# A transformer step with three sequence mixers: both softmax maps of the differential attention side by side, two sets of query and key tiles, projections and recurrence products in another order

## Chip, cores and metric

One core of one Trainium2 chip runs the whole program. The metric is the device time of one execution in microseconds (us). "Row halves" are partitions 0 to 63 and 64 to 127 of TensorE's array: a matmul that contracts over 64 rows needs one of them only.

## What is computed

1024 positions, width 1024, fp32. Block 1 projects the modulated, normalised input `h` onto 6688 columns. They feed three mixers, whose outputs are projected, gated and added; an output projection and a dense MLP follow. Block 2 (softmax attention and a mixture of experts) isn't touched.

```python
# mixer A: 4 heads, each with two maps of 64 dimensions; v has 128 columns
scores = einsum('bhiqd,bhikd->bhiqk', q, k) * 64**-0.5      # i = 0, 1: the two maps
scores = scores - slopes * abs(t - s)
p = softmax(scores, axis=-1)
o = (p[:, :, 0] - lam * p[:, :, 1]) @ v                      # then an RMS norm

# mixers B (4 heads of 64) and C (4 heads of 32 for keys, 64 for values), in both directions
S_t = diag(a_t) S_{t-1} + k_t v_t^T ;  o_t = S_t^T q_t

# merge: a gate for each branch, 3 * 1024 of the projected columns
m = sigmoid(gA) * (oA @ WA) + sigmoid(gB) * (oB @ WB) + sigmoid(gC) * (oC @ WC)
```

## The kernel before, in words

Every product of projections and scores is made in three passes: an operand is split into a rounded fp32r part (`hi`, ScalarE) and its remainder (`lo`, VectorE), and hi·hi, hi·lo and lo·hi are added up in PSUM (`mm3`, L91 to L93). Weights arrive by DMA (`wraw`) and are split (`whi` L98, `wlo` L99). PSUM has eight banks: `mm` is two buffers of two banks (tiles named `ps`, `pA`, `mm`), `mb` takes one half of an `mm` buffer, `tp` has two single banks, **`po` and `pj` one bank each, with a single buffer**: their tiles are handed out in the order in which the code asks for them, and each waits until the one before it has been read.

The code is written as a program of tiles; a scheduler orders each engine's instructions by priorities, from dependencies and modelled costs. What is written inside `low_priority()` fills the gaps that the rest leaves on an engine, as far as its buffers allow.

Block 1 up to the output projection, in the order of the code:

- **Branch A** (`branch_a` L405, `diff_head` L453). For each pair of heads the values are projected (`proj_N2`, tiles `dv`), for each head 128 query and 128 key columns (`proj_T2`, two halves of 512 positions, an `mm` buffer). `q_stack` (L361, L362) writes query hi and lo one above the other on the 128 partitions (`daq`, one tile for each map), `k_stack` (L369 to L373) key hi and lo, with the copies that stacking wants done by 16 DMAs from SBUF to SBUF (L371, L373, `dak`). A map's scores are then hi·hi + lo·hi in one matmul over K=128 (L379) and hi·lo in a second (L381), for each half of 512 keys: four matmuls for each map and each of the eight blocks of 128 queries, t. Then, on VectorE, the distance penalty with a running maximum (L466), ScalarE's exponential (L469), VectorE's combination of the two maps (L476), TensorE's transposes (L396), their split (L98, L99), the product with the values into `po`, a norm (ones matmul L490 into `po`), and a store (L493).
- **Branch B** (`branch_b`): values by `proj_V`, then two groups of two heads. A group projects its query, gate and two forget columns (`proj_T2`, four `mm` buffers), makes log decays and their running sums (L538, L540), and calls `scan_group` (L545): decayed products of queries and keys on TensorE (`products`, L555), once for the whole and at seven levels of chunk lengths 64 to 1, each over the group's heads one after the other; the levels' operands are made on VectorE (L571 to L582), ScalarE (L575, L576) and GpSimd (L577), and each product is merged into a tile `A` per head by a predicated copy on VectorE (L584). States (L612, L616), outputs (L631, L635) and a norm (`head_norm_gate`, L647 into `po`) follow.
- **Branch C** (`branch_c`): the same with four heads of 32 in one group; its rank-16 gate is `plr`, `pz` (L729).
- **Gates and merge** (`mid()`, called in `branch_c`, but in `low_priority`): `gate_cols` projects the 24 blocks of 128 gate columns through `pj`, copies them to `gst` (L791) and stores them in DRAM. `merge_ab` projects the outputs of A and B (`pj<-oT`), with VectorE multiplying by the gate (L818) straight from `pj`. `merge_c` (`mm<-oC`) and the output projection (`mb<-whi,mT`) follow.

Of the kernel before, what the change touches and what calls it, by code (L numbers as in the profile page):

```python
# [26 lines left out]
class Kern:  # L27
# [379 lines left out]
    def branch_a(self, hT, oa, first):  # L407
        nc, tc, a = self.nc, self.tc, self.a
        W = a["w_in"]
        with ExitStack() as ctx:  # L410
# [24 lines left out]
            for hp in range(2):  # L435
                vt = [sp.tile([128, NT, 256], FR, name="dv%d" % i, tag="dv%d" % i) for i in range(2)]
                self.proj_N2(self.w256(W, 1024 + hp * 256) if hp else first, hT, lambda t2, p: self.split_into(
                    p, *[x[:, 2 * t2:2 * t2 + 2, :] for x in vt]), self.mb)
                for h in (2 * hp, 2 * hp + 1):
                    Q = [sp.tile([128, 1024], FR, name="daq%d" % i, tag="daq%d" % i) for i in range(2)]  # L440
                    KK = [[sp.tile([128, 1024], FR, name="dak%d%d" % (i, j), tag="dak%d%d" % (i, j))
                           for j in range(2)] for i in range(2)]
                    p = self.proj_T2(self.w128(W, h * 128), hT)
                    for i in range(2):
                        self.q_stack(p[64 * i:64 * i + 64], 64 * i, Q[i], -0.125)
                    p = self.proj_T2(self.w128(W, 512 + h * 128), hT)
                    for i in range(2):
                        self.k_stack(p[64 * i:64 * i + 64], 64 * i, *KK[i])
                    nc.vector.tensor_scalar(tab, tab, 0.25, None, op0=ALU.mult)
                    self.diff_head(sp, Q, KK, [x[:, :, (h % 2) * 128:(h % 2) * 128 + 128] for x in vt],  # L450
                                   tab, nlam, ones, gcol, oa, h)

    def diff_head(self, sp, Q, KK, V, tab, nlam, ones, gcol, oa, h):  # L453
        nc = self.nc
        for qr in range(4):
            pt = self.pt_tiles(sp, 2)
            rc = sp.tile([128, 2], F32, name="drc", tag="drc", bufs=2)
            for qi in range(2):
# [3 lines left out]
                for i in range(2):  # L462
                    p = self.mm("ps")
                    self.scores(p, Q[i], KK[i][0], KK[i][1], t)
# [77 lines left out]
    def scan_group(self, sp, q, kf, kb, cf, cb, V, nh, escale, out):  # L542
# [6 lines left out]
        A = [sp.tile([128, 8, 128], F32, name="A%d" % h, tag="A%d" % h) for h in range(nh)]  # L549
# [11 lines left out]
        products(xk, q, lambda h, p: nc.scalar.activation(A[h], p, AF.Copy))  # L561
# [1589 lines left out]
```

## Time and profile before

| | us |
|---|---|
| three runs | 4387.36, 4399.77, 4403.98 (median 4399.77) |
| the profiled execution | 4400.4 |
| its span | 4398.6 |
| TensorE busy | 3972.5 (90%) |
| VectorE / ScalarE / GpSimd busy | 2367.1 / 1837.5 / 1149.5 |
| from the first head's projections to the end of `mm<-oC` | 93 to 1281 |

Matmuls overlap in TensorE's pipeline, so a row's duration is longer than the distance to the next start; a row in the timeline with x8 is a run of eight. What a matmul costs is the distance between starts: 0.234 us for 512 columns of fp32r at the full clock. An fp32 product of 128 columns has two records. The granted clock (PEclk) is a share of full speed.

### The profile page before, as it was taken

How to read it: one execution, taken by the hardware profiler on the slowest of the kernel's cores; microseconds unless marked ns; L12 is line 12 of the kernel's file. 1: busy time of each engine (PE TensorE's matmuls, PEld its weight loads, DVE VectorE, ACT ScalarE, POOL GpSimd, SP SyncE). 2: the span in 40 equal slices, each digit the busy share in tenths (PEclk: the TensorE clock that was granted, in tenths of full speed). 3: DMA queues.
4: the chain of work that ended last, by engine and by line, in shares of the span. 5: the costliest groups of instructions: out<-in, count | busy, mean ns of one | idle time of the engine just before them, and what ended most of it. 6: DMA issues, size and time to landing. Idle time of an engine off the chain costs nothing. (4 is left out here: it accounts for less than half of the span.)

```text
span 4398.6 us, 56718 instructions
## 1 busy us (share of the span) xinstructions
PE 3972.5 (90%) x21637; PEld 3280.9 (75%) x21637; DVE 2367.1 (54%) x3984; ACT 1837.5 (42%) x3064; POOL 1149.5 (26%) x878
## 2 busy tenths in 40 slices
PE   6999989989989999999899988699795988996997
PEld 5788867768768888887799987566594877884664
DVE  6545575544544233334536674666438567746665
ACT  3444432523233212121436662255423667842554
POOL 2000021322153212123522221011124646730111
PEclk8999989877799999999899998799996999997998
DMA  4222251102152211112233323699610001036996
GB/s 165 60 61 66 80 181 39 54 20 95 60 200 82 63 44 53 44 53 68 76 99 80 94 85 105 256 369 360 194 42 15 19 8 57 20 100 254 370 362 226
DMA packets 314163, 514.32 MB, mean 117 GB/s; under 512 B 39318, under 2 KB 212769, under 8 KB 313892
## 3 DMA queue, kind: packets, MB, share of 16 engines
q1 hardware_dynamic: 304244, 475.58, 32.0%
q0 software_dynamic: 9648, 35.13, 3.2%
q8 instruction: 170, 2.79, 0.3%
q14 instruction: 101, 0.83, 0.1%
HBM read 418.87 MB, written 83.36 MB: 114 GB/s over the span
## 5 line engine op out<-in xcount | busy, mean ns | idle before, releaser
L98 ACT ACTIVATE whi<-wraw 128x1024 fp32r<-128x1024 f32 (+3 forms) x451 | 465.3, 1035 | 929.2 <-PE mm L92 258.7
L99 DVE TENSOR_TENSOR wlo<-wraw,whi 128x1024 fp32r<-128x1024 f32 (+1 forms) x354 | 450.9, 1277 | 635.6 <-ACT whi L98 607.8
L99 POOL TENSOR_TENSOR wlo<-wraw,whi 128x1024 fp32r<-128x1024 f32 (+3 forms) x97 | 227.8, 2349 | 1227.8 <-ACT whi L98 1157.4
L91 PE MATMUL mm<-h,whi 128*128 128x512 f32 x832 | 331.5, 400 | 8.0 <-DVE xq L649 4.2
L92 PE MATMUL mm<-h,whi 128*128 128x512 f32 x832 | 331.6, 399 | 2.9 <-POOL h L99 1.8
L93 PE MATMUL mm<-h,wlo 128*128 128x512 f32 x832 | 331.4, 399 | 1.1 <-POOL wlo L99 1.1
L1619 PE MATMUL pd<-wraw,se 128*128 128x512 f32 x512 | 237.3, 598 | 1.9 <-ACT se L1611 1.9
L91 PE MATMUL pgu<-whi,xe 128*128 128x512 f32 x512 | 216.4, 423 | 5.3 <-ACT xe L98 5.3
L92 PE MATMUL pgu<-wlo,xe 128*128 128x512 f32 x512 | 216.4, 423 | 0.0
L91 PE MATMUL py<-whi,mr 128*128 128x512 f32 x512 | 201.6, 394 | 9.2 <-DVE mr L921 8.1
L912 DVE TENSOR_TENSOR Y<-py,Y 128x1024 f32<-128x1024 f32 x112 | 137.0, 1224 | 133.4 <-PE py L93 133.4
L93 PE MATMUL pgu<-whi,xe 128*128 128x512 f32 x512 | 204.3, 399 | 0.0
L93 PE MATMUL py<-whi,mr 128*128 128x512 f32 x512 | 203.1, 397 | 0.0
L92 PE MATMUL py<-wlo,mr 128*128 128x512 f32 x512 | 202.4, 395 | 0.0
L396 PE MATMUL ptp<-ident,e 128*128 128x128 f32 x1280 | 181.9, 277 | 11.8 <-ACT pf L400 5.1
L91 PEld LDWEIGHTS mm<-h,whi 128*128 128x128 f32 x832 | 156.9, 189 | 47.7 <-issue 5.3
L1023 DVE TENSOR_REDUCE ast<-ps 128x1 f32<-128x1024 f32 x128 | 156.4, 1222 | 66.4 <-PE ps L93 47.1
L92 PEld LDWEIGHTS mm<-h,whi 128*128 128x128 f32 x832 | 157.2, 189 | 41.6 <-POOL h L99 2.3
L93 PEld LDWEIGHTS mm<-h,wlo 128*128 128x128 f32 x832 | 157.4, 189 | 40.2 <-POOL wlo L99 2.0
L91 PE MATMUL pj<-h,whi 128*128 128x512 f32 x384 | 160.0, 417 | 17.6 <-ACT gst L791 17.5
L396 PEld LDWEIGHTS ptp<-ident,e 128*128 128x128 f32 x1280 | 148.9, 142 | 27.0 <-ACT pf L400 11.6
L1619 PEld LDWEIGHTS pd<-wraw,se 128*128 128x128 f32 x512 | 97.6, 191 | 95.2 <-issue 84.3
(625 smaller groups left out, 11111.4 us busy)
## 6 DMA issues: line engine op xcount, KB each, us to landing
wraw<-in_moe_w_gate_dram SPq DMA_DIRECT2D x128, 512.0 KB
wraw<-in_moe_w_up_dram SPq DMA_DIRECT2D x128, 512.0 KB
wraw<-in_moe_w_down_dram SPq DMA_DIRECT2D x128, 512.0 KB
wraw<-in_mlp_w_dram SPq DMA_DIRECT2D x64, 512.0 KB
wraw<-in_w_in_dram SPq DMA_DIRECT2D x52, 512.0 KB
wad<-in_ada_w_dram SPq DMA_DIRECT2D x48, 512.0 KB
gD<-gst SPq DMA_DIRECT2D x24, 512.0 KB
wraw<-x SPq DMA_DIRECT2D x20, 512.0 KB
```

Source lines behind the costliest of these rows:

```text
L91: t.matmul(out, l[0], r[0], start=start, stop=False)
L92: t.matmul(out, l[0], r[1], start=False, stop=False)
L93: return t.matmul(out, l[1], r[0], start=False, stop=stop)
L98: nc.scalar.activation(hi, src, AF.Copy)
L99: (nc.gpsimd if leng == "pool" else nc.vector).tensor_tensor(lo, src, hi.bitcast(F32), op=ALU.subtract)
L396: nc.tensor.transpose(p[:, k, :], e[:, (4 * kg + k) * 128:(4 * kg + k + 1) * 128], self.ident)
L912: nc.vector.tensor_tensor(y, pv, y, op=ALU.add)
L1023: nc.vector.tensor_reduce(out=st[:, 0:1], in_=pv, axis=AX.X, op=ALU.min)
L1619: nc.tensor.matmul(p[:, h, :], sT[:, k, :], w[:, h * 512:(h + 1) * 512], start=k == 0, stop=k == 3)
```

## The change

1. Branch A: queries and keys of a head lie as they come out of the projection, map 0 on partitions 0 to 63 and map 1 on 64 to 127, as one hi and one lo tile each, two sets in rotation. `q_stack`, `k_stack` and their 16 DMAs go. The scores become three matmuls over K=64 for each half of 512 keys, written alternately for the two maps. Projections of heads 1 to 3 and of the second pair's values go through `pj` instead of `mm`.
2. `early()`, in low priority and ahead of branch A in the code: all projections of B and C (2080 columns) go through `pj` and `gst` to DRAM, and the branches load them by DMA.
3. `products`: heads in pairs, alternating, four chunks at a time; the four or two tiles `A` become one.
4. `merge_ab`: the first of two halves in `po`, the second in `pj`.

```diff
 # branch_a
-                    p, *[x[:, 2 * t2:2 * t2 + 2, :] for x in vt]), self.mb)
+                    p, *[x[:, 2 * t2:2 * t2 + 2, :] for x in vt]), self.pj if hp else self.mb)
                 for h in (2 * hp, 2 * hp + 1):
-                    Q = [sp.tile([128, 1024], FR, name="daq%d" % i, tag="daq%d" % i) for i in range(2)]
-                    KK = [[sp.tile([128, 1024], FR, name="dak%d%d" % (i, j), tag="dak%d%d" % (i, j))
-                           for j in range(2)] for i in range(2)]
-                    p = self.proj_T2(self.w128(W, h * 128), hT)
-                    for i in range(2):
-                        self.q_stack(p[64 * i:64 * i + 64], 64 * i, Q[i], -0.125)
...
+                    Q, K = [[sp.tile([128, 1024], FR, name="da%s%d" % (n, i), tag="da%s%d" % (n, i), bufs=2)
+                             for i in range(2)] for n in "qk"]
+                    for c0, T, s in ((0, Q, -0.125), (512, K, 1.0)):
+                        w = self.w128(W, c0 + h * 128)
+                        for g in range(2):
+                            p = self.pj() if h else self.mb()
+                            self.proj_T(w, hT, p, g)
+                            hi, lo = [x[:, g * 512:(g + 1) * 512] for x in T]
+                            nc.scalar.activation(hi, p, AF.Copy, scale=s)
+                            nc.vector.scalar_tensor_tensor(lo, p, s, hi.bitcast(F32), op0=ALU.mult, op1=ALU.subtract)
 # diff_head
-                for i in range(2):
-                    p = self.mm("ps")
-                    self.scores(p, Q[i], KK[i][0], KK[i][1], t)
+                ps = [self.mm("ps") for _ in range(2)]
+                for kh in range(2):
+                    for n, (x, y) in enumerate(((0, 0), (0, 1), (1, 0))):
+                        for i in range(2):
+                            hs = slice(64 * i, 64 * i + 64)
+                            nc.tensor.matmul(ps[i][:, kh, :], Q[x][hs, t * 128:(t + 1) * 128],
+                                             K[y][hs, kh * 512:(kh + 1) * 512], start=n == 0, stop=n == 2)
+                for i, p in enumerate(ps):
 # scan_group
-            for h in range(nh):
-                p = self.mm("pA").rearrange("p a (c j) -> p (a c) j", j=128)
-                for c in range(8):
-                    nc.tensor.matmul(p[:, c, :], xk[h * dk:(h + 1) * dk, c * 128:(c + 1) * 128],
-                                     xq[h * dk:(h + 1) * dk, c * 128:(c + 1) * 128], start=True, stop=True)
-                done(h, p)
+            for h in range(0, nh, 2):
+                for g in range(0, 8, 4):
+                    p = self.mm("pA").rearrange("p a (c j) -> p a c j", j=128)
+                    for c in range(4):
+                        for i in range(2):
+                            hs, cs = slice((h + i) * dk, (h + i + 1) * dk), slice((g + c) * 128, (g + c + 1) * 128)
+                            nc.tensor.matmul(p[:, i, c, :], xk[hs, cs], xq[hs, cs], start=True, stop=True)
+                    done(A[:, h:h + 2, g:g + 4, :], p)
 # branch_b (branch_c in the same way)
-            self.proj_V(self.w256(W, 2304), hT, V)
+            self.load_V(vD, V)
...
-                p = self.proj_T2(self.w128(W, 1536 + 128 * i), hT)
-                nc.scalar.activation(q, p, AF.Silu)
+                nc.scalar.activation(q, load(q, 0, i), AF.Silu)
 # merge_ab
-                    p = self.pj()
+                    p = self.pj() if h else self.po()
 # program; store_rows and store_cols project through pj, copy to gst on ScalarE, and store
+        def early():
+            self.store_rows(h, vB, 2304, sf, W)
+            for i in range(2):
+                for k, c in enumerate((1536, 1792, 2048, 2560)):
+                    self.store_cols(h, pB[256 * k + 128 * i:256 * k + 128 * i + 128, :], c + 128 * i, sf, W)
+            self.store_cols(h, pC[512:544, :], 3584, sf, W, 32)
+            for k, c in enumerate((2816, 2944, 3328, 3456)):
+                self.store_cols(h, pC[128 * k:128 * k + 128, :], c, sf, W)
+            self.store_rows(h, vC, 3072, sf, W)
+        with self.low_priority():
+            early()
         self.branch_a(h, oD, first)
```

**The scores on TensorE.** Before, in head 0 (`ps` the scores, `dak` and `daq` keys and queries, `pj` low-priority projections); four matmuls for one map, one block of queries:

```order
L93 MATMUL pj_5525<-h10_97,wlo_5495 128x512
L379 MATMUL ps_919<-dak00_639,daq0_637 128x512
L381 MATMUL ps_919<-dak01_640,daq0_637 128x512
L379 MATMUL ps_919<-dak00_639,daq0_637 128x512
L381 MATMUL ps_919<-dak01_640,daq0_637 128x512
L91 MATMUL pj_5525<-h10_97,whi_5494 128x512
```

Now, at the same place; `ps_2027` is map 0 on the lower row half, `ps_2028` map 1 on the upper:

```order
L93 MATMUL pj_480<-whi_424,h11_98 128x256
L470 MATMUL ps_2027<-dak0_1859,daq0_1857 128x512
L470 MATMUL ps_2027<-dak1_1860,daq0_1857 128x512
L470 MATMUL ps_2027<-dak0_1859,daq1_1858 128x512
L470 MATMUL ps_2027<-dak0_1859,daq0_1857 128x512
L470 MATMUL ps_2027<-dak1_1860,daq0_1857 128x512
L470 MATMUL ps_2027<-dak0_1859,daq1_1858 128x512
L470 MATMUL ps_2028<-dak0_1859,daq0_1857 128x512
L470 MATMUL ps_2028<-dak1_1860,daq0_1857 128x512
L470 MATMUL ps_2028<-dak0_1859,daq1_1858 128x512
L470 MATMUL ps_2028<-dak0_1859,daq0_1857 128x512
L470 MATMUL ps_2028<-dak1_1860,daq0_1857 128x512
```

The matmuls that the code writes alternately stand as six of one map and then six of the other. So it is in most blocks of queries; in others the two maps' runs are parted by low-priority work, and in a few they alternate. In the whole order the 384 score matmuls lie in 52 unbroken runs, with 94 changes from one half to the other inside them.

**The end of head 0 on TensorE.** Before, the projections of head 1 (`mm_1285`) stand around the last norm of head 0 (L490):

```order
L92 MATMUL mm_1285<-h11_98,whi_1281 128x512
L93 MATMUL mm_1285<-h10_97,wlo_1282 128x512
L490 MATMUL po_1177<-dsq_1205,ones_426 128x256
L91 MATMUL mm_1285<-h10_97,whi_1281 128x512
L92 MATMUL mm_1285<-h11_98,whi_1281 128x512
```

Now tiles of `early()`, `pj_727` and then `pj_761` to `pj_1581`, stand between head 0 and head 1 (its last norm is L498); the rows are head 0's last product with the values and what follows it:

```order
L93 MATMUL po_2425<-pt0_2344,dv1_1652 128x256
L491 MATMUL po_2425<-ident_74,drc_2346 128x128 x2
L91 MATMUL pj_727<-h10_97,whi_696 128x512
L92 MATMUL pj_727<-h11_98,whi_696 128x512
L93 MATMUL pj_727<-h10_97,wlo_697 128x512
```

From head 0's last norm on, 528 matmuls of 512 columns and 192 of 256 columns (the second V of `early()`), all into `pj`, stand there before the first projection of head 1, with nothing between them; 72 more of 512 columns, head 1's own projections, precede its first score.

**The end of branch C on TensorE.** Before, the norms (L647) stand among the merge's `pj<-oT`, as soon as their outputs are there:

```order
L91 MATMUL pj_7221<-oT0_6876,whi_7200 128x512
L92 MATMUL pj_7221<-oT1_6880,whi_7200 128x512
L647 MATMUL po_7932<-xq_7925,bones_4885 128x512
L93 MATMUL pj_7221<-oT0_6876,wlo_7201 128x512
L91 MATMUL pj_7221<-oT0_6876,whi_7200 128x512
```

Now all four of them (L658) stand behind the merge's last product, right ahead of `mm<-oC`:

```order
L93 MATMUL pj_7572<-oT0_7084,wlo_7527 128x512
L658 MATMUL po_8133<-xq_8130,bones_5576 128x512
L658 MATMUL po_8137<-xq_8130,bones_5576 128x512
L658 MATMUL po_8180<-xq_8177,bones_5576 128x512
L658 MATMUL po_8184<-xq_8177,bones_5576 128x512
L91 MATMUL mm_8220<-oC0_8201,whi_8211 128x512
```

`merge_ab` is asked for before the recurrence of C in the code, and now holds turns of `po`: the norms come after all of them. From the output projection on, both orders are the same but for a few swaps of neighbours.

## Rows read from the trace of the kernel before

**Rows 1.** Busy time of each engine by stage (start:end in us, length; then busy us and instructions of PE, PEld, DVE, ACT, POOL; PEclk, DMA share, GB/s): head 0's projections, branch A, then for B's first and second group: setup, levels, states and outputs; the same for C; the merge; `mm<-oC`.

```profile
93.00:123.00 30.00, 27.97 (x121) 22.18 (x120) 6.12 (x5) 6.63 (x8) 2.36 (x1) 1.00 0.28 76
123.00:533.00 410.00, 403.37 (x2202) 343.24 (x2201) 222.77 (x381) 184.42 (x320) 27.51 (x11) 1.00 0.21 60
533.00:645.00 112.00, 99.26 (x466) 80.83 (x464) 79.33 (x95) 34.20 (x39) 30.60 (x14) 0.92 0.65 203
645.00:714.00 69.00, 60.51 (x367) 52.47 (x367) 55.76 (x56) 20.37 (x22) 21.54 (x9) 0.87 0.13 39
714.00:759.00 45.00, 43.49 (x218) 33.76 (x218) 13.15 (x33) 7.29 (x11) 2.73 (x2) 0.93 0.16 48
759.00:832.00 73.00, 67.46 (x279) 52.38 (x279) 22.49 (x36) 38.49 (x42) 26.28 (x11) 0.98 0.19 60
832.00:887.00 55.00, 49.18 (x284) 45.64 (x283) 47.73 (x52) 23.25 (x23) 15.64 (x7) 0.66 0.09 29
887.00:918.00 31.00, 26.57 (x104) 18.73 (x102) 11.24 (x31) 3.44 (x5) 0.00 (x0) 0.50 0.00 1
918.00:1020.00 102.00, 92.60 (x451) 71.25 (x448) 34.75 (x54) 28.98 (x31) 32.17 (x15) 0.92 0.13 38
1020.00:1152.00 132.00, 127.23 (x615) 109.53 (x613) 79.75 (x74) 44.27 (x44) 26.41 (x11) 0.62 0.23 81
1152.00:1207.00 55.00, 51.08 (x258) 36.33 (x258) 25.95 (x69) 13.84 (x15) 10.74 (x5) 0.96 0.25 84
1207.00:1249.00 42.00, 33.62 (x127) 23.34 (x128) 14.45 (x16) 22.40 (x25) 16.68 (x8) 0.96 0.55 207
1249.00:1281.00 32.00, 23.50 (x83) 17.56 (x82) 20.01 (x17) 14.88 (x18) 21.34 (x11) 0.84 0.73 251
```

**Rows 2.** TensorE's groups between 50 and 1300 us, shapes apart (line, engine, operation, out<-in, rows x columns of the array, xcount | busy us, mean ns | idle before, releaser).

```profile
L91 PE MATMUL mm<-h,whi 128*128 128x512 f32 x320 | 129.3, 404 | 6.7 <-DVE xq L649 4.2 <-ACT hq L675 1.8 <-ACT whi L98 0.7
L379 PE MATMUL ps<-dak,daq 128*128 128x512 f32 x128 | 52.9, 414 | 5.6 <-DMA dak<-dak 5.2 <-DVE dst L466 0.4
L381 PE MATMUL ps<-dak,daq 128*128 128x512 f32 x128 | 50.5, 397 | 0.8 <-DMA dak<-dak 0.7
L396 PE MATMUL ptp<-ident,e 128*128 128x128 f32 x256 | 34.8, 272 | 0.0
L555 PE MATMUL pA<-xq,xk 64*128 64x128 f32 x448 | 69.0, 345 | 7.7 <-DVE xk L582 5.8 <-DVE A L584 1.8
L555 PE MATMUL pA<-xq,xk 32*128 32x128 f32 x448 | 77.1, 369 | 4.5 <-DVE A L584 4.5
```

**Rows 3.** TensorE's timeline (start us, length us, engine, line, operation, run; idle before and releaser in brackets) at four places: scores and transposes; low-priority projections with a `pj` tile's end and the next one's start in between, twice; and the start of B's products.

```profile
141.31 0.39 PE L379 MATMUL ps<-dak,daq 128*128 128x512 f32 x1
141.53 0.39 PE L381 MATMUL ps<-dak,daq 128*128 128x512 f32 x1
141.76 0.39 PE L379 MATMUL ps<-dak,daq 128*128 128x512 f32 x1
...
142.91 1.04 PE L396 MATMUL ptp<-ident,e 128*128 128x128 f32 x8
143.71 0.48 PE L379 MATMUL ps<-dak,daq 128*128 128x512 f32 x1
...
623.20 0.40 PE L93 MATMUL pj<-h,wlo 128*128 128x512 f32 x1
624.28 0.50 PE L91 MATMUL pj<-h,whi 128*128 128x512 f32 x1 [0.69 <-ACT gst L791]
...
822.63 0.40 PE L93 MATMUL pj<-h,wlo 128*128 128x512 f32 x1
824.88 0.50 PE L91 MATMUL pj<-h,whi 128*128 128x512 f32 x1 [1.85 <-ACT gst L791]
...
644.61 0.40 PE L93 MATMUL pj<-h,wlo 128*128 128x512 f32 x1
644.94 1.04 PE L555 MATMUL pA<-hq,xk 64*128 64x128 f32 x7
```

**Rows 4.** TensorE's timeline in B's first group: where the second head's products of one level (`hq`, upper row half) meet the next level's first (`xq`, lower row half), at about half the clock; in the program every `hq` row here stands ahead of every `xq` row. And B's outputs, products over 128 rows (L631) alternating with 64-column halves of the array (L635).

```profile
658.41 0.58 PE L555 MATMUL pA<-xq,xk 64*128 64x128 f32 x1
658.62 0.42 PE L555 MATMUL pA<-hq,xk 64*128 64x128 f32 x1
658.79 0.42 PE L555 MATMUL pA<-xq,xk 64*128 64x128 f32 x1
658.84 0.42 PE L555 MATMUL pA<-hq,xk 64*128 64x128 f32 x1
659.00 0.42 PE L555 MATMUL pA<-xq,xk 64*128 64x128 f32 x1
659.05 0.42 PE L555 MATMUL pA<-hq,xk 64*128 64x128 f32 x1
659.22 0.42 PE L555 MATMUL pA<-xq,xk 64*128 64x128 f32 x1
...
752.45 0.44 PE L635 MATMUL pO<-A,hv 128*64 128x128 f32 x4
752.82 0.71 PE L631 MATMUL pO<-qd,st 128*128 128x128 f32 x4
```

**Rows 5.** The groups of VectorE (columns as in rows 2) that one block of queries passes through in branch A, 120 to 535 us; then, for C's levels, 1019 to 1151 us, the merging of products.

```profile
L466 DVE CUSTOM_DVE_ANT_0 e<-ps,dist 128x1024 f32<-128x1024 f32 x64 | 77.8, 1222 | 40.1 <-PE ps L381 34.5 <-PE ptp L396 4.3
L99 DVE TENSOR_TENSOR pt<-ptp,pt 128x512 fp32r<-128x512 f32 x64 | 42.3, 684 | 15.5 <-ACT pt L98 15.5
L476 DVE SCALAR_TENSOR_TENSOR e<-e,dst,e 128x1024 f32<-128x1024 f32 x32 | 41.1, 1284 | 1.0
...
L584 DVE COPY_PREDICATED A<-lm,pA 128x1024 f32<-128x1024 uint8 x27 | 34.7, 1298 | 28.3 <-PE pA L555 28.0
```

**Rows 6.** ScalarE's copy of a `pj` tile (duration ns min/median/max), and the end of the program's longest norm tail, the last norm of C and the matmul behind it.

```profile
L791 ACT ACTIVATE gst<-pj x48: 575/597/602, 116.6 to 845.2; 128x512 f32<-128x512 f32 x48
...
1214.79 1.93 PE L647 MATMUL po<-xq,bones 128*128 128x512 f32 x2 [2.37 <-ACT xk L498]
1215.73 1.42 PE L91 MATMUL pj<-oT,whi 128*128 128x512 f32 x1
```

More of the change, by code (lines that the diff above doesn't have):

```diff
@@ L548, in scan_group @@
         nv = nh * 64
-        A = [sp.tile([128, 8, 128], F32, name="A%d" % h, tag="A%d" % h) for h in range(nh)]
+        A = sp.tile([128, nh, 8, 128], F32, name="A", tag="A")
         def products(xk, xq, done):
-            for h in range(nh):
-                p = self.mm("pA").rearrange("p a (c j) -> p (a c) j", j=128)
-                for c in range(8):
-                    nc.tensor.matmul(p[:, c, :], xk[h * dk:(h + 1) * dk, c * 128:(c + 1) * 128],
-                                     xq[h * dk:(h + 1) * dk, c * 128:(c + 1) * 128], start=True, stop=True)
-                done(h, p)
+            for h in range(0, nh, 2):
[6 more added lines that the diff above has]
+                    done(A[:, h:h + 2, g:g + 4, :], p)
         xk = sp.tile([128, 1024], F32, name="xk", tag="xk", bufs=2)
         nc.gpsimd.tensor_tensor(xk, kf, kb, op=ALU.add)
-        products(xk, q, lambda h, p: nc.scalar.activation(A[h], p, AF.Copy))
+        products(xk, q, lambda a, p: nc.scalar.activation(a, p, AF.Copy))
         L = 64
@@ L635, in scan_group @@
                     nc.tensor.matmul(p[64 * h:64 * h + 64, c, :], V[:, c, (2 * j + h) * 64:(2 * j + h + 1) * 64],
-                                     A[2 * j + h][:, c, :], start=False, stop=True)
+                                     A[:, 2 * j + h, c, :], start=False, stop=True)
             out(j, p.rearrange("p c j -> p (c j)"))
@@ L651, in head_norm_gate, with load_V, branch_b, load @@
         nc.sync.dma_start(dst[row:row + 128, :], sq)
-    def proj_V(self, w, hT, V):
-        self.proj_N2(w, hT, lambda t2, p: self.nc.vector.tensor_copy(V[:, 2 * t2:2 * t2 + 2, :], p), self.mb)
-    def branch_b(self, hT, dst):
+    def load_V(self, src, V):
+        self.nc.sync.dma_start(V, dap(src, 0, [[256, 128], [128 * 256, 8], [1, 256]]))
+    def branch_b(self, pD, vD, dst):
         nc, tc, a = self.nc, self.tc, self.a
-        W = a["w_in"]
+        def load(t, k, i):
+            r = 256 * k + 128 * i
+            nc.sync.dma_start(t, pD[r:r + 128, :])
+            return t
         with tc.tile_pool(name="hb", bufs=1) as sp:
@@ L685, in branch_b @@
                     la.append(l)
-                    z = self.proj_T2(self.w128(W, 1792 + 256 * d + 128 * i), hT)
+                    z = load(sp.tile([128, 1024], F32, name="hz", tag="xq", bufs=2), 1 + d, i)
                     l2 = self.softplus_neg_abs(z, sp)
@@ L711, in branch_c @@
             lr = sp.tile([32, 1024], F32, name="glr", tag="xk", bufs=2)
[L712 to L716 removed]
+            nc.sync.dma_start(lr, pD[512:544, :])
             q = sp.tile([128, 1024], F32, name="gq")
[L718 to L719 removed]
+            nc.sync.dma_start(q, pD[0:128, :])
+            nc.scalar.activation(q, q, AF.Copy, scale=32.0 ** -0.5)
             k_ = sp.tile([128, 1024], F32, name="gk")
[L721 to L722 removed]
+            nc.sync.dma_start(k_, pD[128:256, :])
             self.exp_ln_table()
@@ L789, in gate_cols, with store_rows, evac @@
             p = self.pj()
-            self.proj_T(wl, hT, p, h)
-            nc.scalar.activation(s[:, h * 512:(h + 1) * 512], p, AF.Copy)
-        nc.sync.dma_start(gD[j * 128:(j + 1) * 128, :], s)
+            self.proj_T(wl, hT, p[0:m, :], h)
+            nc.scalar.activation(s[0:m, h * 512:(h + 1) * 512], p[0:m, :], AF.Copy)
+        nc.sync.dma_start(dst, s[0:m, :])
+    def store_rows(self, hT, dst, c0, sp, W):
+        nc = self.nc
+        wl = self.w256(self.a["w_in"], c0, W)
+        s = sp.tile([128, 1024], F32, name="gst", tag="gst", bufs=2)
+        def evac(t2, p):
+            if t2 == 2:
+                s2.append(sp.tile([128, 1024], F32, name="gst", tag="gst", bufs=2))
+            x = s2[-1][:, t2 % 2 * 512:t2 % 2 * 512 + 512].rearrange("p (u m) -> p u m", u=2)
+            nc.scalar.activation(x, p, AF.Copy)
+            nc.sync.dma_start(dap(dst, 2 * t2 * 128 * 256, [[256, 128], [128 * 256, 2], [1, 256]]), x)
+        s2 = [s]
+        self.proj_N2(wl, hT, evac, self.pj)
     def up(self, nm, nk, j):
@@ L1883, in program @@
         sf = opn("fl")
+        W = (sf, 1, 2)
+        pB, pC = self.dtile("pB"), self.dtile("pC", 544)
+        vB, vC = [self.dram.tile([1024, 256], F32, name=n) for n in ("vB", "vC")]
+        def early():
[9 more added lines that the diff above has]
+            early()
         self.branch_a(h, oD, first)
@@ L1887, in program @@
             self.ada(s, sp, "wad", 2, self.po)
[L1888 removed]
+        self.branch_b(pB, vB, oD)
         cls("ad")
```

42 lines of the change are left out of this document (13 added, 29 removed).

## The prediction

> **What bounds the kernel now.** I first read the busy times by stage [rows 1]. From the first scores to branch A's end (123 to 533 us) TensorE is busy 403 of 410 us at clock 1.00 and VectorE 223: TensorE is the bound. Counted in the built order at the distances between starts in the timeline [rows 3] (0.23 us for 512 columns, 0.11 for a transpose and for half an fp32 product of 128 columns), its matmuls there come to 403 us: no room, every matmul added or removed there is paid in full. From 533 to 1281 us the same count is 554 us in 748: some 190 us of room. Three things eat it. The setups (533 to 645, 759 to 832, 918 to 1020) are projections with chains of elementwise work behind them. B's levels are VectorE's (56 and 48 us busy in 69 and 55). C's levels, 132 us, show TensorE busy 127 us, but at a clock of 0.62, with VectorE at 80 us. What is short work there is long because of the clock and because the products of K=64 and K=32 use a half or a quarter of the rows (448 and 448 records, with 5.8 and 4.5 us of waiting on VectorE) [rows 2]. From the output projection on both orders are the same, so the change of the whole is the change of the point at which `mm<-oC` ends, 1281 us.
>
> The groups of TensorE [rows 2] then tell which of its work the change touches: 256 score matmuls (L379, L381), the projections `mm<-h`, and the products L555; those of VectorE [rows 5] what a head costs it.
>
> **The change, part by part.**
>
> *Scores.* 256 matmuls × 0.23 = 59 us become 384. The row halves can work side by side: at 658.62 to 659.22 the products of the two halves start 0.05 and 0.16 us apart in turn, a pair in 0.21, where one alone takes 0.21 at that clock; and an `xq` row starts at 658.41, ahead of `hq` rows that precede it in the program [rows 4]. Fully side by side, 384 would take 44 us. But the built order mostly has six of one map and then six of the other. I walked through it three ways: without any overlap 384 × 0.231 = 89 us; where only neighbours pair, 326 turns, 75 us; where up to three may be overtaken, 294 turns, 68 us. To that comes the entry into the half-array form and out of it. A row bounds it from one side: the first product over 64 rows starts 0.33 us behind the matmul before it, not 0.23 [rows 3], and the change from half-width products to full ones costs nothing visible beyond that (752.45 to 752.82, four records in 0.37) [rows 4]; so 0.1 to 0.3 us for each of 52 runs, 5 to 16 us, and I take 13. I take 75 + 13 = 88: +29 us, with +14 and +46 as ends. This part loses.
>
> By the Trainium skill ("TensorE: Matmul & The Clock Gate", Part 3) matmuls start and end strictly in program order; rows 4 show one start ahead of its turn, so here the trace decides, and by the rule alone the scores would cost 75 us and the entries, which is what I took. Its page "TensorEngine Tiling (Array Packing)" (Tiling Modes, Key Properties) says that changing the tiling mode drains the engine; it gives no price, the rows' 0.1 us is what can be seen of it.
>
> *Stacking.* The 16 DMAs and the half-tile splits go; the waits that they cost TensorE are 5.2 + 0.7 us [rows 2]. Each head now has four ScalarE copies (0.6 us, by the same size in rows 6) and four VectorE splits (0.68, as L99 in rows 5) of half tiles; both engines have room in branch A [rows 1]. Worth −6 us, which the low-priority work had partly covered: −4.
>
> *Early projections in the single bank `pj`.* This is the largest shift. 720 matmuls, 528 × 0.233 + 192 × 0.117 = 145 us, stand between head 0's last norm and head 1 with nothing between them, and 17 us of head 1's own projections follow; heads 1 to 3 can't begin before the turns of `pj` ahead of theirs are over. In such a stretch each tile waits for ScalarE's copy of the one before. Two of these gaps: 623.20 to 624.28 and 822.63 to 824.88, where a free bank would give 0.23, so 0.85 and 2.0 us lost, of which the copy is 0.6 [rows 3, 6]. The second had ScalarE busy with other work; in the early stretch it only has copies and weight splits, so I take 1.15 us × 27 tiles = 31 us, with 23 and 54 as ends. Then the stretch from the first score to branch A's end: matmuls 487 us by the same count of the new order (scores at 89), −1 for pairing less entries (88 for 89), 31 for the gaps, 10 for other starts (2%, as 403 in 410 before), 5 for head 1, whose 57 us of matmuls hardly exceed VectorE's 8 blocks at 5.1 to 7.0 us (2 × 1.22 + 2 × 0.68 + 1.28 [rows 5], or 223 / 32 [rows 1]). The first score comes at 93 + 96 × 0.233 + 41 × 0.117 = 120. Branch A ends at 120 + 487 − 1 + 31 + 10 + 5 = about 652, not 533: **+119 us**. Of the 16 MB of other weights that stream meanwhile nothing changes.
>
> *Branches B and C without projections, and their products in pairs.* Against the stages of rows 1, in their order: first setup 112 → 45 (34 us of matmuls remain in the order, all low-priority; the chain to the first product is loads and elementwise work): −67. First levels 69 → 62, bound by VectorE at 56: −7. States and outputs 45 → 42. Second setup 73 → 35: −38. Second levels 55 → 60, filled with gates now: +5. States 31 → 42, filled as well: +11. C's setup 102 → 50: −52. C's levels 132 → 90: half of the 512 records' time for products goes, and VectorE's 80 us becomes the bound; the clock of 0.62 went with the half-empty array and not with idleness, and gates still fill the first half of this stage: −42, with 0 and −52 as ends. States 55 → 59: +4. Merge 42 → 27: −15, since ten more of its halves precede. Then the tail: all four norms of C come behind the last of `merge_ab` in `po`'s turns, so what was hidden under `pj<-oT` (the chain with 2.37 us of waiting [rows 6], then GpSimd's multiplication, the store, the load and split of `oC`) lies open: 20 us, with 8 and 30 as ends. `mm<-oC` 32 → 31. Together −67 −7 −3 −38 +5 +11 −52 −42 +4 −15 +20 −1 = **−185 us**.
>
> *Sum.* +119 − 185 = −66; I take −60, as the fillers run out half way through C. On the profiled execution's 4400.4 us (0.6 us above the median of the runs, 4399.8) that is **4340 us**; with the ends of gaps, scores and C's levels, 4312 to 4372.
>
> **Rivals.**
> - *The fill holds* (4290 us). B and C together hold 505 us of matmuls from branch A's end on, some 455 if half of the products pair. If TensorE ran at 0.9 there (it was 0.98 in branch A), they would take 506 us and not 563, and scores that overtake give 7 back: −57 − 7, some 4280 to 4300. For it: the order has gates ready through most of that time. Against: VectorE's levels and the chains of the setups, which no filler shortens.
> - *The gain is eaten up* (4390 us). The gaps at 2.0 us cost 23 more, the scores without pairs 13 more, and C's levels, 132 → 118 instead of 90, 28: −60 + 64 is no change. What speaks for it: the clock was 0.50 to 0.66 in B's second levels and states as well [rows 1], and no row of before shows a longer run of products in pairs.
> - *The halves don't run side by side* (4431 us, slower). Rows 4 show pairs at one place, at half the clock, where two products came from different steps. If the array at full clock takes one at a time, or each change of half costs an entry, scores cost 89 + 13, products give back none of their 50 us, and C stays at TensorE's limit: −60 + 14 + 50 + 27 = +31. It decides from an average distance of about 0.2 us between score matmuls up.
> - That the change doesn't do what it says is true of the scores already: the order undoes most of the interleaving that the code writes.
>
> **Chances.** Forecast 0.55, fill 0.20, no gain 0.17, slower 0.08. The range leaves out the slower case and the outer part of the fill: 4268 to 4396. A measurement of this kernel tells some 0.5%, 22 us, from no change: faster 0.76 (forecast, fill, and a piece of the third case), the same 0.17, slower 0.07.
>
> **What would show it.** Branch A's last norm near 650 us, after a stretch of `pj<-h` alone of 165 to 190 us without scores; VectorE nearly idle in it. `pj` tiles 1.1 to 2.2 us apart at their ends. Scores at a mean distance under 0.2 us where they alternate and 0.23 where six stand together. B's first product within 50 us of branch A's end, C's levels in 80 to 100 us at a higher clock, the norms L658 last, and idle TensorE of some 20 us ahead of `mm<-oC`; that ends near 1220. If branch A ends before 600, or B and C take longer than 620, the account is wrong.

## The result, and the profile after

4432.45 us (median of 5 runs, 4426.28 to 4435.44) against 4399.77: ratio 1.0069, 95% interval 1.0054 to 1.0084. The change is **slower by 0.7%**; 4340 was forecast, and the range ended at 4396. The profiled execution's span is 4433.7 us. `mm<-oC` is done and the output projection starts at 1308 us, not 1281 and not the forecast 1220. That is 28 of the 35 us between the profiled executions; the other 7 lie behind that point, in the same order of instructions, where the traces of the runs in the table below have 3114 to 3127 us. Sums by stage and times therefore agree only within some 10 us.

Stages of the changed kernel (columns of [rows 1]), cut at the same events as there: head 0's projections, branch A, B's first setup, levels, states and outputs, second setup, levels, states and outputs, C's setup, levels, states and outputs, the last norms, the tail; then branch A and all behind it.

```profile
93.00:112.00 19.00, 19.00 (x87) 15.32 (x85) 2.08 (x3) 2.74 (x4) 2.41 (x1) 1.00 0.09 28
112.00:677.00 565.00, 511.16 (x2705) 403.54 (x2703) 215.99 (x386) 193.23 (x342) 32.86 (x14) 0.98 0.15 47
677.00:733.00 56.00, 40.55 (x164) 31.12 (x164) 43.86 (x60) 27.44 (x33) 21.39 (x11) 0.90 0.58 199
733.00:810.00 77.00, 60.37 (x408) 49.60 (x406) 72.25 (x75) 21.20 (x23) 26.69 (x8) 0.81 0.48 151
810.00:864.00 54.00, 47.53 (x242) 37.38 (x243) 25.31 (x44) 13.14 (x19) 7.00 (x4) 0.93 0.40 127
864.00:912.00 48.00, 38.71 (x147) 28.76 (x147) 26.75 (x34) 36.18 (x40) 23.32 (x10) 0.93 0.32 99
912.00:965.00 53.00, 44.85 (x356) 36.01 (x357) 46.80 (x50) 19.07 (x21) 17.90 (x7) 0.90 0.13 41
965.00:1008.00 43.00, 41.65 (x224) 32.78 (x223) 14.54 (x34) 8.71 (x13) 4.74 (x2) 1.00 0.23 74
1008.00:1046.00 38.00, 35.57 (x133) 25.25 (x131) 13.33 (x28) 18.15 (x21) 13.03 (x8) 0.96 0.45 152
1046.00:1164.00 118.00, 99.54 (x677) 78.02 (x677) 87.88 (x86) 60.51 (x62) 33.07 (x13) 0.73 0.25 91
1164.00:1224.00 60.00, 60.00 (x323) 47.21 (x323) 30.47 (x77) 15.76 (x18) 18.03 (x8) 1.00 0.43 143
1224.00:1259.00 35.00, 27.01 (x103) 19.30 (x102) 11.36 (x15) 14.78 (x17) 12.25 (x6) 0.88 0.33 116
1259.00:1308.00 49.00, 27.26 (x98) 19.06 (x96) 25.94 (x17) 25.40 (x30) 25.53 (x12) 0.77 0.73 258
93.00:677.00 584.00, 530.16 (x2790) 418.86 (x2788) 218.07 (x389) 195.97 (x346) 35.27 (x15) 0.98 0.15 47
677.00:1308.00 631.00, 523.03 (x2862) 404.51 (x2860) 398.51 (x515) 260.34 (x292) 202.95 (x85) 0.87 0.38 129
```

Branch A is 144 us longer than before and everything behind it 117 us shorter: 584 + 631 = 1215 for 440 + 748 = 1188. TensorE is busy 1053 us here, before 1106: it lost its saturation, in branch A too (530 of 584).

TensorE's groups between 93 and 1308 us (columns of [rows 2]):

```profile
L91 PE MATMUL pj<-h,whi 128*128 128x512 f32 x672 | 287.9, 428 | 64.1 <-ACT gst L799 53.1 <-DVE daq L450 8.2 <-DVE dv L99 1.4
L470 PE MATMUL ps<-dak,daq 64*128 64x512 f32 x384 | 84.6, 414 | 6.4 <-ACT dak L449 2.9 <-DVE dst L474 1.8 <-DVE dak L450 1.8
L567 PE MATMUL pA<-xq,xk 32*128 32x128 f32 x448 | 38.8, 328 | 7.0 <-DVE A L595 7.0
L567 PE MATMUL pA<-xq,xk 64*128 64x128 f32 x448 | 36.7, 320 | 23.3 <-DVE A L595 20.6 <-DVE xk L593 2.7
```

Its waits in the same stretch (who waited for whom, us in total, times, longest us):

```profile
PE pj L91 <- ACT gst L799: 57.0, 42, 6.8
PE pA L567 <- DVE A L595: 27.7, 9, 7.0
PE mm L91 <- ACT oC L98: 14.9, 1, 14.9
PE pj L91 <- DVE daq L450: 8.2, 4, 2.5
```

Against [rows 2]: the products' busy time is halved (77.1 to 38.8, 69.0 to 36.7), so pairs run side by side; the 384 scores take 85 us. What is new is the wait for `gst`: 57 us, where `pj<-h` waited 17.5 before. The timeline shows one such wait in the stretch without scores, and three forms of the scores: six of one half alone, twelve alternating, and six of one half ahead of six of the other:

```profile
308.14 0.40 PE L93 MATMUL pj<-h,wlo 128*128 128x512 f32 x1
309.98 0.50 PE L91 MATMUL pj<-h,whi 128*128 128x512 f32 x1 [1.44 <-ACT gst L799]
...
130.73 1.66 PE L470 MATMUL ps<-dak,daq 64*128 64x512 f32 x6
132.31 0.38 PE L91 MATMUL pj<-whi,h 128*128 128x256 f32 x1
...
165.40 1.67 PE L470 MATMUL ps<-dak,daq 64*128 64x512 f32 x12
167.00 0.49 PE L92 MATMUL pj<-h,whi 128*128 128x512 f32 x1
...
170.35 2.23 PE L470 MATMUL ps<-dak,daq 64*128 64x512 f32 x12
172.51 0.50 PE L91 MATMUL pj<-h,whi 128*128 128x512 f32 x1
```

To the next start the six at 130.73 take 1.58 us, the twelve that alternate at 165.40 take 1.60, and the twelve at 170.35, six and six, 2.16. So where they alternate, the second half's six come for nothing. Eight of before took 8 × 0.23 = 1.85 [rows 3].

### The profile page after: what moved, and what is told of

The parts are those of the page before. It is cut to its first block, busy times and chain, and to the rows that moved or that the text cites. A ratio compares the mean times of both kernels' runs of the same rounds, so it can differ in the third digit from the quotient of the medians.

```text
span 4433.7 us, 57025 instructions
## 1 busy us (share of the span) xinstructions
PE 3925.1 (89%) x21765; PEld 3202.7 (72%) x21765; DVE 2347.1 (53%) x3974; ACT 1849.8 (42%) x3101; POOL 1158.9 (26%) x878
## 5 line engine op out<-in xcount | busy, mean ns | idle before, releaser
L91 PE MATMUL pj<-h,whi 128*128 128x512 f32 (+1 forms) x688 | 294.2, 428 | 66.5 <-ACT gst L799 55.6
L92 PE MATMUL pj<-h,whi 128*128 128x512 f32 (+1 forms) x688 | 284.6, 414 | 0.0
L93 PE MATMUL pj<-h,wlo 128*128 128x512 f32 (+1 forms) x688 | 283.6, 412 | 0.1
L91 PEld LDWEIGHTS pj<-h,whi 128*128 128x128 f32 (+1 forms) x688 | 134.9, 196 | 126.5 <-ACT gst L799 74.6
L92 PE MATMUL mm<-h,whi 128*128 128x512 f32 x512 | 203.4, 397 | 2.9 <-POOL h L99 1.8
L93 PE MATMUL mm<-h,wlo 128*128 128x512 f32 x512 | 203.0, 397 | 0.8 <-POOL wlo L99 0.8
L91 PE MATMUL mm<-h,whi 128*128 128x512 f32 x512 | 202.5, 398 | 1.4 <-ACT ms L913 1.4
L402 POOL TENSOR_TENSOR pt<-pf,pt 128x512 fp32r<-128x512 f32 x128 | 165.6, 1294 | 10.6
```

The lines of the kernel that those rows point to most:

```text
L91: t.matmul(out, l[0], r[0], start=start, stop=False)
L92: t.matmul(out, l[0], r[1], start=False, stop=False)
L93: return t.matmul(out, l[1], r[0], start=False, stop=stop)
L402: nc.gpsimd.tensor_tensor(lo, f, hi.bitcast(F32), op=ALU.subtract)
```

## The experiments

A's end and the start of the output projection, with `mm<-oC` done, are from each run's trace; ratios are to the kernel before.

| run | median us | ratio, 95% | A ends | output projection starts |
|---|---|---|---|---|
| before / changed | 4399.8 / 4432.5 | 1.0069 (1.0054 to 1.0084) | 533 / 677 | 1281 / 1308 |
| pairs alone | 4361.3 | 0.9918 (0.9902 to 0.9934) | 532 | 1238 |
| K=64 scores alone | 4389.2 | 0.9987 (0.9978 to 0.9996) | 507 | 1263 |
| K=64 scores, heads in pj | 4402.6 | 1.0011 (0.9998 to 1.0025) | 436 | 1292 |
| no early | 4327.9 | 0.9840 (0.9825 to 0.9854) | 433 | 1202 |
| no early, heads in mm | 4364.1 | 0.9928 (0.9914 to 0.9943) | 507 | 1238 |
| early, heads in mm | 4372.1 | 0.9943 (0.9928 to 0.9958) | 506 | 1247 |
| early in mm | 4417.1 | 1.0041 (1.0028 to 1.0054) | 658 | 1292 |
| early behind the heads | 4425.2 | 1.0068 (1.0055 to 1.0082) | 435 | 1303 |
| early for C only | 4371.2 | 0.9934 (0.9922 to 0.9947) | 528 | 1241 |

### One part alone, and the square of early and the heads' bank

Pairs alone is the kernel before with `scan_group` of the change; K=64 scores alone has its branch A, but

```diff
-                    ... self.pj if hp else self.mb)
+                    ... self.mb)
-                            p = self.pj() if h else self.mb()
+                            p = self.mb()
```

> The kernel before with part 3 alone (recurrence products of two heads in turn, one tile A). If products of two heads run side by side, C's levels fall from 135 us to 100 to 110 and B's second levels from 55 to 50: 4360 to 4370 us. If VectorE's merging or the half clock is what holds C's levels, they stay over 120: 4385 to 4400.

> The kernel before with the new query and key tiles and the scores over K=64, projections still through mm. My account of the scores (86 us in place of 59, stacking's DMAs saved) makes branch A 20 to 27 us longer, all of it on the path: 4420 to 4427 us. If the two sets let heads overlap and hide it, 4395 to 4405.

Pairs save 33 us, as expected: C's levels, from the first product to the last, take 103 us and not 132.

```profile
1009.00:1112.00 103.00, 84.05 (x619) 66.59 (x617) 76.16 (x72) 44.39 (x44) 26.22 (x11) 0.70 0.30 104
```

The scores alone lie under both forecasts: 30 us more of TensorE's work, and no loss. Their branch A and all behind it, and the gates in branch A (one of their three passes), before and in this run:

```profile
93.00:507.00 414.00, 414.00 (x2281) 335.24 (x2280) 213.49 (x384) 175.05 (x317) 26.38 (x11) 1.00 0.16 47
507.00:1263.00 756.00, 688.97 (x3397) 552.43 (x3396) 404.88 (x530) 250.34 (x275) 207.01 (x89) 0.87 0.30 96
...
L91 PE MATMUL pj<-h,whi 128*128 128x512 f32 x230 | 92.8, 403 | 2.2 <-ACT gst L791 2.0
L91 PE MATMUL pj<-h,whi 128*128 128x512 f32 x174 | 72.1, 414 | 0.0
```

Next, no early (B and C project for themselves, as before), and the changed kernel with the edit above:

> The changed kernel without early(): branches B and C project for themselves as before; K=64 scores, projections of heads 1 to 3 through pj, pairs and the merge's po stay. If early() in the single bank is the loss, this is 30 to 50 us below the changed kernel: 4385 to 4400. If the loss lies in the scores and in po's turns, it stays within 15 us of the changed kernel: 4420 to 4445.

> The changed kernel, but the projections of heads 1 to 3 and of the second values go through mm again; early() keeps pj for itself. If the loss comes from the heads' place behind early() in pj's turns, the stretch without scores (206 us) goes, early() fills under heads 0 to 3, and branch A ends at 620 to 635 us, not 677: 4375 to 4395. If TensorE's work and VectorE's levels are the loss, wherever the projections lie, 4420 to 4435.

> The run without early(), with the projections of heads 1 to 3 through mm again: with the runs before it, early() and the heads' bank make a square of four. If early() costs by itself, because it takes out of B and C what filled their gaps, this is 20 to 35 us below the run with early() and the heads in mm (4372): 4340 to 4352 us. If it costs only by standing ahead of the heads in pj, this is at 4365 to 4380.

The stages of three of the four, branch A and all behind it (columns of [rows 1]; the changed kernel's stand above). No early:

```profile
93.00:433.00 340.00, 322.62 (x1850) 259.48 (x1849) 204.64 (x380) 157.18 (x290) 14.34 (x6) 0.99 0.10 30
433.00:1202.00 769.00, 685.53 (x3831) 537.84 (x3829) 413.20 (x535) 258.24 (x295) 219.39 (x94) 0.94 0.33 107
```

No early, heads in mm:

```profile
93.00:507.00 414.00, 414.00 (x2278) 335.18 (x2277) 213.53 (x384) 175.05 (x317) 26.39 (x11) 1.00 0.16 47
507.00:1238.00 731.00, 620.44 (x3403) 483.48 (x3402) 408.62 (x530) 258.73 (x282) 211.38 (x89) 0.88 0.31 99
```

Early, heads in mm:

```profile
93.00:506.00 413.00, 412.22 (x2307) 332.94 (x2305) 213.58 (x385) 177.02 (x321) 25.89 (x11) 1.00 0.15 46
506.00:1247.00 741.00, 611.17 (x3342) 477.86 (x3340) 413.83 (x520) 268.28 (x308) 215.74 (x89) 0.90 0.37 121
```

No early comes in under both of its forecasts, and with early() and the heads in mm branch A ends far ahead of the 620 to 635 us expected. With the heads in mm, early() costs 8 us, with intervals that overlap: it takes the place of the gates as filler of a branch A that is 413 us either way, and the gates take its place behind. With the heads in pj it costs 104. Without early(), the heads in pj *save* 36 us: ahead of the gates in the bank's turns, they push some 100 us of gates out of branch A, which ends 74 us earlier, and B and C take them in for 38 more. Is that the same without pairs? The run moves the K=64 scores' heads into pj:

> The run with the K=64 scores alone (4389), but with heads 1 to 3 projected through pj, ahead of the gates in its turns. If low-priority work costs in branch A what it takes, and nothing in B and C, pushing some 90 us of gates out of branch A makes that stage 70 to 80 us shorter and the whole 4355 to 4370 us. If the waits for the single bank eat it, 4385 to 4400.

```profile
93.00:436.00 343.00, 325.62 (x1849) 262.01 (x1848) 204.68 (x380) 157.27 (x290) 14.35 (x6) 0.99 0.10 29
436.00:1292.00 856.00, 768.88 (x3831) 610.50 (x3830) 404.42 (x534) 263.70 (x298) 222.99 (x95) 0.91 0.30 96
```

It isn't: in the trace branch A is 71 us shorter and the rest 100 us longer (756 to 856). That execution is the slowest of twelve, 4386 to 4420 us; by the ratios the sum is 0.2% slower, outside both forecasts. My account of it fell. Of the 75 us between this run and no early, the merge's second bank is worth 26 (no early with the merge in `pj` alone, below) and the pairs the other 49; that these two make room in B and C for the gates fits, but isn't shown by itself.

### Where early's price lies

Early() called behind branch A (its turns of pj then come after the heads'); early() through the two mm buffers; early() for C alone:

```diff
+        self.branch_a(h, oD, first)
         with self.low_priority():
             early()
-        self.branch_a(h, oD, first)
```

> The changed kernel with early() called behind branch A in the code, so that its turns of pj come after those of heads 1 to 3 and ahead of the gates'. If the loss is early()'s place ahead of the heads in the turns of the one bank, heads 0 and 1 end near 192 and 241 us as in the run without early(), and the whole is at 4320 to 4350 us. If early() itself is the loss (copies, stores and loads, work taken out of branches that have room), 4370 to 4410. If both count for little, 4420 to 4440.

> The changed kernel with early() through the two mm buffers: it runs as one block ahead of head 0, without the single bank's waits and ahead of no head in pj. Branch A's end moves from 677 us to 433 (as without early()) plus 182 us of matmuls, some 620. If the part of early()'s price that lies in branch A is the bank's and the heads' waiting, the whole falls by about that, to 4370 to 4385 us. If what was saved in branch A is lost in B and C again, 4415 to 4440.

> The changed kernel with only C's projections (800 of 2080 columns) in early(); B projects for itself as before. If early()'s price of 104 us is the waiting of heads 1 to 3 behind it and the matmuls taken out of the gaps of B and C, it goes with the columns: 4328 + 40, so 4360 to 4380 us. If C's stage had no gaps that its projections could fill, and B's had, 4320 to 4345.

Stages of the run with early behind the heads (columns as above): branch A, then up to C's outputs, a stretch of gates alone, the merge and the tail.

```profile
93.00:435.00 342.00, 324.45 (x1882) 262.95 (x1880) 205.16 (x380) 158.67 (x291) 13.79 (x6) 0.99 0.10 28
435.00:967.00 532.00, 449.07 (x2738) 351.62 (x2736) 348.29 (x460) 201.18 (x230) 139.55 (x60) 0.91 0.32 101
967.00:1165.00 198.00, 164.20 (x676) 123.81 (x672) 7.34 (x6) 33.30 (x45) 14.32 (x6) 1.00 0.25 76
1165.00:1303.00 138.00, 103.83 (x392) 77.11 (x392) 62.29 (x58) 62.43 (x68) 63.18 (x28) 0.85 0.64 223
```

Stages of the run with early in mm: up to the first score, branch A, all behind.

```profile
93.00:322.00 229.00, 227.79 (x1217) 189.66 (x1216) 16.57 (x17) 44.39 (x62) 23.92 (x10) 1.00 0.26 81
93.00:658.00 565.00, 544.85 (x2950) 440.14 (x2948) 219.68 (x394) 200.43 (x351) 37.68 (x16) 0.98 0.16 50
658.00:1292.00 634.00, 513.16 (x2861) 398.14 (x2860) 399.33 (x515) 257.52 (x290) 204.26 (x85) 0.89 0.38 129
```

Early behind the heads is as slow as the changed kernel, in the range that the expectation gave to both causes counting for little. Its place ahead of the heads isn't the cause by itself: branch A is free of it (342 us), but now the gates are late, and 198 us of them stand alone behind C's outputs, with VectorE busy 7 us. Early in mm runs without waits (228 of 229 us) and ahead of no head in pj. It saves only 12 us by the ratios, but that isn't the bank's whole price. Its tiles take their turns ahead of head 0's, and TensorE has done less by 93 us:

```profile
0.00:93.00 93.00, 58.96 (x322) 47.97 (x323) 65.42 (x81) 32.47 (x56) 27.96 (x18) 0.78 0.54 190
0.00:93.00 93.00, 42.49 (x163) 29.92 (x164) 62.58 (x76) 29.17 (x51) 25.38 (x17) 0.67 0.51 181
```

Some 21 us of matmuls that the changed kernel (first line) has done by 93 us stand in branch A here. Against no early, branch A takes 225 us more for 210 us of matmuls (counted at their distances), where the changed kernel takes 244 for 188: without the single bank's waits and turns its excess falls from 56 to 15 us. B and C still take 634 us, so their part of the price isn't the bank's. For C alone the price goes with the columns: 43 us for 800 of 2080 (104 × 0.38 = 40).

### The bank, the merge and the other suspects

The copies of `pj` cut in two halves, one on VectorE:

```diff
-            nc.scalar.activation(s[0:m, h * 512:(h + 1) * 512], p[0:m, :], AF.Copy)
+            nc.scalar.activation(s[0:m, h * 512:h * 512 + 256], p[0:m, :256], AF.Copy)
+            nc.vector.tensor_copy(s[0:m, h * 512 + 256:h * 512 + 512], p[0:m, 256:])
```

> The changed kernel with each copy of a pj tile to gst cut in halves, one on ScalarE, one on VectorE, side by side. If the copy's length (0.58 us) is what the next tile waits for, the 42 waits shorten by some 0.25 us each and with them the stages behind: 4415 to 4425 us. If they are ScalarE's queue and the signalling, or VectorE's levels pay for it, 4428 to 4440.

4482.1 us, ratio 1.0193 (1.0179 to 1.0207): worse by 50 us, though each copy is shorter. TensorE's waits for it:

```profile
PE pj L91 <- DVE gst L800: 103.0, 49, 8.6
```

103 us, not 57: in VectorE's order the copies stand behind its long operations. A single bank costs what its reader's queue makes of it. Two banks for `pj` and one for transposes, with and without early():

```diff
-name="pstp", bufs=2 ... name="pspj", bufs=1
+name="pstp", bufs=1 ... name="pspj", bufs=2
```

> The changed kernel with two banks for pj and one for the transposes (tp). If the single bank of pj is why early() loses, the waits for its copies (57 us of TensorE's time between 93 and 1308 us) nearly go and transposes pay for part of it: 4375 to 4400 us. If the loss is in which stage the projections stand, and not in the bank, 4420 to 4445.

> The run without early() (4327.9) with two banks for pj and one for tp. Its waits for copies are 20 us: 4310 to 4330 us if the transposes bear one bank, 4335 to 4360 if they don't. If the bank explains early()'s price, the two-bank run with early() comes within 60 us of this one, not 104.

4836.9 and 4795.7 us, 1.0994 and 1.0908, far outside every forecast: one bank for transposes costs the whole program over 400 us. Early's price is 41 us in this pair, under the 60 that the expectation set as the sign of the bank. But branch A without early() ends at 585 us here, not at 433, and so has room that early() can fill; the pair doesn't separate the two. The merge in `pj` alone, in the changed kernel and without early (`p = self.pj()`):

> The changed kernel with merge_ab in pj alone, as before. If the norms of C lose by standing behind the merge in po's turns (11 us between them and 16 us of idle TensorE behind the last), the end of mm<-oC comes 15 to 25 us earlier: 4407 to 4417 us. If the second bank gives the merge as much as that costs, 4425 to 4440.

> The run without early() with merge_ab in pj alone as well: K=64 scores, heads 1 to 3 in pj, and pairs remain of the change. If po's turns cost what the trace without early() shows (11 us between the norms and 15 us of idle TensorE behind the last), 4303 to 4313 us. If the merge needs its second bank, 4325 to 4345.

4442.0 (1.0103, 1.0088 to 1.0119) and 4353.8 (0.9899, 0.9884 to 0.9914): `po`'s part is a gain of 0.3 and 0.6%, not the loss that I had made of it. The norms in a `tp` bank:

```diff
-            ps = self.po()
+            ps = self.tp("pn").rearrange("p a b -> p (a b)")
```

> The changed kernel with the norm's sums (L658) in a tp bank, so that C's norms don't stand behind the merge in po's turns. If that tail (11 us between the norms, 16 behind them) is lost time, 4403 to 4412 us. If the merge or the gates set the end in any case, 4425 to 4435.

> The run without early() (4328) with the norm's sums in a tp bank: the merge keeps its two banks and C's norms come as soon as their outputs are there. 11 us between the norms and 15 us behind them are idle in that run: 4300 to 4308 us. If the merge's own work sets the end, 4322 to 4332.

4425.9 (1.0067, 1.0052 to 1.0081) and 4324.5 (0.9836, 0.9821 to 0.9851), against 1.0069 and 0.9840 with the norms in `po`: no difference that can be told. Last, the 16 MB of `ada` weights, of whose operations on VectorE 14 of 1.3 us and three of 0.74 fell into B's first levels (32 between 685 and 830 us):

```diff
-        for s in range(2, 6):
-            self.ada(s, sp, "wad", 2, self.po)
         self.branch_b(pB, vB, oD)
+        for s in range(2, 6):
+            self.ada(s, sp, "wad", 2, self.po)
```

> The changed kernel with the 16 MB of ada weights (32 VectorE operations of 0.7 to 1.3 us) called for behind branch B in the code, not ahead of it. If they lengthen B's first levels, which are bound by VectorE and took 87 us in place of 77, those levels fall to 65 to 72 us and the whole to 4410 to 4420 us. If VectorE's time there is covered by TensorE's low-priority work, or the operations only move to C's levels, 4425 to 4440.

> The changed kernel with the accumulation of the ada weights taken off VectorE in the same place: ScalarE multiplies (32 times 1.05 us), GpSimd adds (28 times 2.4 us). If those operations on VectorE lengthen B's first levels (87 us, 61 in the run that has them later), the levels fall to 62 to 70 us and the whole to 4408 to 4420. If GpSimd's load or TensorE's work takes their place, 4425 to 4440.

Called later, B's first levels shrink by more than expected, from 77 to 52 us, but C's setup grows from 38 to 110 us and C's levels from 118 to 134, and the whole is 4470.9 (1.0166, 1.0152 to 1.0180), above both forecasts. Taken off VectorE (`nc.scalar.activation(w, w, AF.Identity, scale=...)` and a GpSimd addition), 4424.8 (1.0070, 1.0055 to 1.0085): no difference, though B's first levels are 71 us there. So on VectorE they lengthen a stage and not the kernel.

No early is the best version, with or without the norms in `tp`: 4328 and 4325 us, 1.6% under the kernel before.

## Why the prediction was wrong

**What was right.** The scores' price on TensorE: 88 us were forecast; from each run's first start to the next instruction behind it they take 86. In part that is luck: 6 of the 86 are waits and some 10 entries and exits (52 runs at 0.2), which leaves about 70 for the turns, where 75 was taken and the walk with up to three overtaken gave 68. Six and six are 0.18 us apart, where 0.23 was expected. That pairs of products run side by side was right too: alone they save 33 us. The third rival's mechanism is refuted, although its 4431 us is the time that came: twelve alternating scores take what six take, and the products' busy time is halved. The sign that it named, a mean distance of 0.2 us between scores, didn't separate anything: measured are 86 / 384 = 0.22, and the forecast's own 88 us would be 0.23.

**The step that failed: "Together −185 us" for B and C**, with the claim ahead of it that in branch A every matmul is paid in full and behind it there are 190 us of room. Measured: −117; B and C take 631 us, over the 620 that the prediction itself named as the sign of a wrong account. Counted at their distances at the full clock (an estimate, each product by itself), the matmuls from 93 us to the output projection are 990 us with early and 993 without, 504 and 316 of them in branch A, 486 and 677 behind. So the 106 us between 1308 and 1202 is no work, only waits and clock: branch A takes 244 us more for 188 of work, and the rest gives back 138 for 191. Early() moved work that cost 0.7 us per us to where it costs 1.3. The forecast let each stage of B and C shrink to its VectorE time or its chain and kept the low-priority work dense in what remained. Measured: first setup 56 for 45, first levels 77 for 62, states and outputs 54 for 42, second setup 48 for 35, second levels 53 for 60, C's setup 38 for 50, and, the largest, C's levels 118 for 90.

C's levels are also where most of the 53 us is lost that early() doesn't get back. The changed kernel's row, 1046 to 1164 us, stands above; without early() they are:

```profile
927.00:1010.00 83.00, 80.82 (x713) 64.40 (x712) 66.73 (x61) 28.79 (x33) 14.26 (x6) 0.98 0.19 56
```

Without early() gates stand between the products, TensorE is busy 81 of the 83 us and VectorE 67, and the granted clock is 0.98. In the changed kernel they are 35 us longer for 8 us less of matmuls: VectorE, ScalarE and GpSimd have 21, 32 and 19 us more to do there, TensorE stands idle for 18 us, and the granted clock is 0.73. With pairs alone it is 0.70, in the kernel before 0.62. B's first levels are 77 us for 60, with 7 us more of matmuls.

**Branch A**, 677 for 652: from head 0's last norm to head 1's first score, 198 to 404 us, are 206 us, where 145 + 17 + 31 = 193 were forecast, and head 1 took 74 us for 57 + 5 = 62, with no filler but values whose copies wait in turn. These are the 25 us. In the stretch the waits for the copies of `pj` to `gst`, as distances beyond 0.23 us, came to 33 us, near the forecast 31; not forecast were 5 us of waits for head 1's own splits (`daq`).

**The claim of saturation** fell with the K=64 scores alone. In branch A 161 us of gates ran before (`pj<-h`); with 30 us more of scores, 39 us of gates moved behind A, where they filled gaps: A ends 26 us earlier, the rest is 8 us longer. A stage that is full of low-priority work is no bound by that work.

**The tail**, +20: the idle time was there (14.88 us ahead of `mm<-oC`, where 20 were forecast), but norms taken out of `po`'s turns gave nothing that can be told, so as a term it was worth about nothing. The `po` turns, which I counted as loss alone, bring more by the merge's second bank.

The rival "the gain is eaten up" was nearest in kind, and its largest term came true to the microsecond: C's levels at 118 us, 28 us over the forecast. Its other two did not: the gaps came to 33 us, not 54, and the scores to 86. Two rivals are also added up wrongly in the prediction: the terms of this one, −60 + 64, give 4404 us and not 4390, and those of "the fill holds", −57 − 7, give 4276 and not 4290.

**Open.** Which of the differences in C's levels makes them long: the elementwise work that now falls into them, the idle times of TensorE or the clock behind them. That the part of early's price in B and C stays without the bank's waits is shown; no run took one chain of these stages out alone except `ada`, which made no difference.

## What to carry to other kernels

Count TensorE's work in a stage by priority: low-priority filler in a full stage is not a bound, and work taken out of stages with chains saves less there than it costs in a stage that has nothing beside it. Moving work early never paid here: it cost 8 us where it replaced other filler, and 104 where the main work queued behind it. Before a low-priority stream gets a single buffer, look at what its reader's queue holds. Giving the buffer's turns to the main work first is no rule by itself: it saved 36 us in one version and cost 13 in another.

## What the runs showed of the hardware

Matmuls on two row halves run side by side at full clock also when the program has six of one half ahead of six of the other: 2.16 us for twelve, where one after the other they would take 12 × 0.23 = 2.8, and 1.60 where they alternate. If the second six waited for the start of the sixth, eleven distances of 0.23 would be 2.5 us at least. Matmuls of the second half thus start before earlier ones of the first, which contradicts the Trainium skill ("TensorE: Matmul & The Clock Gate", Part 3), by which matmuls start strictly in program order; [rows 4] showed it for fp32 already. Alternating, a pair takes the 0.23 us of one matmul: twelve take 1.60 us and six of one half alone 1.58, both with an entry and an exit of some 0.1 us each beyond 6 × 0.23 = 1.4.
